# One level of Strassen in the second matrix of layer 0's MLP: seven products of sums of quarters, with the sums on VectorE

## The chip, the cores and the metric

The kernel runs on one core of a Trainium2 chip. The metric is the device time of one execution in microseconds (us), 2352.38 us in the median of two runs before the change (2352.35 and 2352.41). The engines that matter here are TensorE (PE in the profile, with its weight loads as PEld), VectorE (DVE), ScalarE (ACT) and the queue of SyncE (SP), which issues the loads.

## The reference, cut to what matters

The program is a chain of a two-layer block on 256 tokens (a dilated attention mixer, a convolution mixer, each with an MLP) and of a second two-layer block that carries 256 context tokens beside the 256 tokens. Everything is float32. The stage that is changed is the MLP of the second block's layer 0, which runs on both streams, so on 512 tokens:

```
def sq_relu_mlp(h, w1, b1, w2, b2):     # in effect
    return square(relu(h @ w1 + b1)) @ w2 + b2
# h: 512 x 1024, w1: 1024 x 4096, w2: 4096 x 1024
x = layer_norm(alpha * x + g2 * sq_relu_mlp(x * (1 + sc2) + sh2, w1, b1, w2, b2), ln2_g, ln2_b)
```

The gates `g`, scales `sc` and shifts `sh` of a layer come from a modulation product `silu(c) @ w_mod[l] + b_mod[l]`, a vector times a 1024 x 6144 matrix, for two vectors (tokens and context).

## The kernel before, in words

**Products.** Each float32 operand is split in two parts, high and low, of the type that TensorE takes; a product is then three matmuls, high by high, high by low and low by high (`mm3`, L350 to L352). A weight is loaded as a 128x1024 tile (`w`, L337): a DMA on SP, the high part by a cast on ACT (L343), the low part by a subtraction on DVE (L344). There are four buffers each for raw, high and low tiles.

**The MLP** (`mlp`, L727). The 4096 hidden features are cut in eight chunks of 512. `up(hc)` computes a chunk's hidden features: four weight tiles, each 24 matmuls over 512 tokens into its own PSUM bank, then on ACT relu with bias (L751) and square (L752), and the split into `hh` (ACT, L431) and `hl` (DVE, L432). `down(hc)` multiplies the chunk by its 512 rows of the second matrix: four weight tiles, for two halves of the output columns (`nn`) and four groups of 128 tokens (`j`), 96 matmuls of 512 columns. The order on PE is `up(0)`, then `up(hc+1)` and `down(hc)` by turns.

**What comes out.** After each chunk the eight PSUM banks of 128x512 are added on DVE to the sums `facc` in SBUF (L1677); in the first chunk ACT copies them (L1675). At chunk 6 the sum is multiplied by the gate and added to the residual (`tail`, L1707 and L1710, on DVE), and at chunk 7 the banks of the last product go the same way; then the layer norm and the start of layer 1 follow (`ready`).

**Side work.** Each call of `w` in this stage runs one step of a list of side work (`spin`, with `side_n` = 1). First in it is the scaling of the residual by `alpha` and its bias rows (L955, L956), then the gate rows; after it the modulation product of layer 1 (`mod(1)`, L877 on). The matrix of that is not multiplied on TensorE: a 512 KB tile is loaded, and DVE multiplies each half of it by a scalar per partition and adds it to `macd` (L892), the first of eight on ACT (L890); a product with ones on TensorE then sums the partitions (L901). A step of it is one load and four such operations. These steps are `pinned`: traced so that on each engine they stand behind the weight tile that was issued last. Before layer 1 starts, what is left of the list is drained.

**Order.** Each engine works its queue in order. The order of the queues is found while the kernel is built, by a planner that steps through the traced program with its own estimate of each duration, and takes what is ready by priority, which is the place in the program.

Of the kernel before, what the change touches and what calls it, by code (L numbers as in the profile page):

```python
# [10 lines left out]
F32 = mybir.dt.float32  # L11
F32R = mybir.dt.float32r
BF16 = mybir.dt.bfloat16
AF = mybir.ActivationFunctionType
ALU = mybir.AluOpType
# [6 lines left out]
P = 128  # L22
KT = D // P
# [201 lines left out]
MT = ((1, 1), (5, 5), (0, 0))  # L225
# [9 lines left out]
MG = ((),(),(),(0,1,2),())  # L235

NTS = (0, 1, 0)


class WT:  # L240
# [12 lines left out]
class K:  # L253
# [262 lines left out]
    def mixer_a(self, cx):  # L516
# [136 lines left out]
        for i, _ in enumerate(project(0)):  # L653
            if i == 4:
# [3 lines left out]
                nc.vector.tensor_copy(maskb.rearrange("p q k -> p (q k)"), mf.rearrange("p a b -> p (a b)"))  # L658
            self.tick(NTS[0])
        with self.behind(), self.queued():  # L660
            for j in range(2):
                nc.sync.dma_start(self.res[2 + j], A["x_n"][j])
        for wv in range(4):
# [3 lines left out]
            while parts:  # L667
                for g in list(parts):
                    if next(g, 0) == 0:
                        parts.remove(g)  # L670
                self.tick(NTS[1] if wv < 3 else NTS[2])
        self.ahead = self.norm("norm2_0")
# [51 lines left out]
        o, n = self.vat[name]  # L724
        return self.vs[:, o:o + n]

    def mlp(self, uh, ul, c0, c1, w1, w2, bias, evac, first, mt, ready=None):  # L727

        nc, n = self.nc, c1 - c0

        def up(hc):
            hh = self.t(self.xm, [P, 4, n], "hh", F32R, bufs=2)
            hl = self.t(self.xm, [P, 4, n], "hl", F32R, bufs=2)
            pre = self.tiles([w1[f, 0] for f in range(4)], uh, ul, c0, c1, first) if hc == 0 else []
            if hc == 0 and bias is not None:
                self.side_n = 1
            for c in range(2):
                r = self.t(self.xm, [P, 2, n], "r", bufs=2)
                if n == 256 and hc:
                    pt = self.ps()  # L740
                    pv = [pt[:, 0:256], pt[:, 256:512]]
                else:
                    pv = [p_[:, 0:n] for p_ in pre[c * 2:c * 2 + 2] or [self.ps() for _ in range(2)]]
                if hc:
                    for f in range(2):
                        self.lin_f(pv[f], self.w(w1[hc * 4 + c * 2 + f, 0], 8, 128), 0, uh, ul, c0, c1)
                if bias is None and hc:
                    nc.scalar.activation(r.rearrange("p f t -> p (f t)"), pt, AF.Relu)
                else:
                    for f in range(2):  # L750
                        nc.scalar.activation(r[:, f, :], pv[f], AF.Relu, bias=0.0 if bias is None else bias(hc * 4 + c * 2 + f))  # L751
                nc.scalar.activation(r, r, AF.Square)  # L752
                self.split(hh[:, c * 2:c * 2 + 2, :], hl[:, c * 2:c * 2 + 2, :], r)
                self.tick(mt[min(hc, 1)])
            return hh, hl

        def down(hc, hid):
            groups = [([nn], range(n // P)) for nn in range(2)]
            if hc == 7 and bias is not None:
                groups = [([0, 1], [j, j + 1]) for j in (2, 0)] if n == 512 else [([0, 1], [j]) for j in range(2)]  # L760
            Ws = {}
            for nns, js in groups:
                pts = {(nn, j): self.ps() for nn in nns for j in js}
                for nn in nns:
                    for kc in range(2):
                        if (nn, kc) not in Ws:
                            Ws[nn, kc] = self.w(w2[nn, hc * 2 + kc], 2, 512)
                        if hc == 7 and n == 512 and nn == kc == 1 and js[0] == 0:
                            self.turn(ux, 2)
                        for j in js:  # L770
                            with self.after_tp():
                                self.lin_t(pts[nn, j], Ws[nn, kc], 0, 512, hid[0], hid[1], j * P, k0=kc * 2, first=kc == 0, last=kc == 1)
                if hc == 7 and n == 512 and js[0] == 0:
                    self.turn(ux, 2)
                for nn in nns:
                    for j in js:
                        evac(j, nn, hc, pts[nn, j])
                if hc == 7 and n == 512:
                    ux = ready(js)
                if hc == 7 and nns == [0]:  # L780
                    self.halfway()
                self.tick(mt[min(hc, 1)])

        hid = up(0)
        for hc in range(8):
            nxt = up(hc + 1) if hc < 7 else None
            down(hc, hid)
            hid = nxt

    def mlp1(self, l, u2=None):  # L790
        nc = self.nc
        uh, ul, rs = self.take_norm()
        if u2 is not None:
            self.ncol, self.up = 512, u2
        else:
            self.ahead = self.norm("norm1_1")
        r2 = self.t(self.xp, [P, 2], "r2", bufs=2)
        nc.vector.tensor_tensor(r2, rs, rs, ALU.mult)

        def evac(j, nn, hc, pt):  # L800
            r = self.res[2 + j][:, nn * 512:nn * 512 + 512]
            nc.vector.scalar_tensor_tensor(out=r, in0=pt, scalar=r2[:, j:j + 1], in1=r, op0=ALU.mult, op1=ALU.add)

        self.mlp(uh, ul, 0, 256, self.A[f"m1_{l}"], self.A[f"m2_{l}"], None, evac, BY_HALVES, MT[l])
# [153 lines left out]
    def residual(self, l, toks, G):  # L958

        ss = sorted({j // 2 for j in toks})  # L960
        with self.pinned():
            ag = self.row(self.A["rows"][l * 6 + 1:l * 6 + 2])
            gb = {s: self.row(self.gbd[l][1 - s:2 - s, 1, :]) for s in ss}
        yield
        for j in toks:
            with self.pinned():
                self.residual_step(self.res[j], ag, gb[j // 2])
            yield
        with self.pinned():
            G.update({s: self.gate_row(l, 1, s) for s in ss})  # L970
        yield

    def residual_x(self):
# [625 lines left out]
    def layer(self, l):  # L1599
        nc, tc, A = self.nc, self.tc, self.A  # L1600
        q0 = self.q0 = 0 if l == 0 else 256
        self.nq = 512 - q0
        toks = [0, 1, 2, 3] if l == 0 else [2, 3]
        prev = None if l == 0 else (l - 1) * 6 + 4
        spill = l == 0
        uh, ul = self.u
# [4 lines left out]
        if spill:  # L1611
            gb = {s: self.row(self.gbd[0][1 - s:2 - s, 0, :], 2) for s in range(2)}
# [7 lines left out]
        with tc.tile_pool(name=f"mix{l}", bufs=1) as self.xq:  # L1620
            acc = self.mixer2(l, uh, ul, toks)
# [9 lines left out]
            with tc.tile_pool(name=f"tl{l}", bufs=1) as self.lp:  # L1631
# [9 lines left out]
                u = self.uT()  # L1641
                aff = self.affine(l, 1, self.vecl(f"ln1_g_{l}", 0, KT), self.vecl(f"ln1_b_{l}", 0, KT))
                G = {s: self.gate_row(l, 0, s, 2) for s in sorted({j // 2 for j in toks})}
                ux = self.make_u([1], aff, *u)
                for n in range(2):
                    Ws, pts = {}, {}
# [17 lines left out]
        with ExitStack() as cx:  # L1664
            self.xm = cx.enter_context(tc.tile_pool(name=f"ff{l}", bufs=1))
            self.lp = self.xm
            uh, ul = u
            G = {}
            self.side.insert(0, self.residual(l, toks, G))
            accs = [self.t(self.xm, [P, D], f"facc{j}") for j in toks]  # L1670

            def evac(j, nn, hc, pt):
                a = accs[j][:, nn * 512:nn * 512 + 512]
                if hc == 0:
                    nc.scalar.copy(a, pt)  # L1675
                elif hc < 7:
                    nc.vector.tensor_tensor(a, pt, a, ALU.add)  # L1677
                if hc >= 6:
                    self.tail(toks[j], nn, a if hc == 6 else pt, G[toks[j] // 2])

            if l:
                self.last = [self.t(self.xm, [P, D], f"fin{i}") for i in range(2)]
                for i in range(2):
                    nc.sync.dma_start(self.last[i], A["rows"][10 + i:11 + i].broadcast_to([P, D]))
            def ready(js):

                if l == 0:
                    if js[0] == 2:
                        self.drain_side()
                        self.start(1)  # L1690
                    self.ln(js)
                    if js[0] == 0:
                        self.u_ctx = self.make_u([0], self.aff, *self.u)
                    return self.make_u([1], self.aff, *self.u)
            self.mlp(uh, ul, q0, 512, A[f"w1_{l}"], A[f"w2_{l}"], lambda f: self.vecl(f"b1_{l}", f), evac,
                     self.by_quarters(self.make_u([0], aff, *u)) + [(0, KT, 0, 256)] if l == 0 else self.by_quarters(), MT[2], ready)
            self.side_n = 0
            if l:
                self.finish()
# [93 lines left out]
```

## Time and profile before

| | |
|---|---|
| median of two runs | 2352.38 us |
| profiled execution, its own time | 2352.55 us |
| its span, first to last instruction | 2350.8 us |
| mean granted TensorE clock | 0.989 |
| PE busy | 2278.8 us (97%) |
| DVE busy | 1712.0 us (73%) |
| ACT busy | 1117.2 us (48%) |
| POOL busy | 68.9 us (3%) |
| moved by DMA | 364.73 MB, mean 155 GB/s |

Busy time is the time in which an engine had at least one instruction under way; consecutive instructions of one engine overlap by part of their durations, so that the spacing of starts, not the duration of one, is what an instruction costs in a full queue. Matmuls are pipelined in the same way. A clock of 1.00 is 2.4 GHz, and 0.50 is 1.2 GHz.

### The profile page before, as it was taken

The numbers are of one execution on the slowest core, as the hardware profiler recorded it, in microseconds if no ns is written. First come the engines' busy times: TensorE is split into PE (matmuls) and PEld (weight loads), VectorE is DVE, ScalarE is ACT, GpSimd is POOL, SyncE is SP. The second block draws the span as 40 slices with busy tenths as digits, with TensorE's granted clock in tenths as the row PEclk, the third lists the DMA queues.
The fourth block names the chain that finished last, engine by engine and source line by source line (L and its number), as shares of the span: only waits on it lengthen the run. The fifth ranks groups of instructions, "written<-read, shape, count | busy, mean of one in ns | idle before, by whom it ended". The sixth has DMA issues, their size and how long they took to land.

```text
span 2350.8 us, 35308 instructions
## 1 busy us (share of the span) xinstructions
PE 2278.8 (97%) x13784; PEld 1967.8 (84%) x13796; DVE 1712.0 (73%) x2779; ACT 1117.2 (48%) x1702; POOL 68.9 (3%) x72
## 2 busy tenths in 40 slices
PE   8999989999999999999999999999999999998997
PEld 7989868889999888778777778888889898787996
DVE  6788878977766668985755777677568778776667
ACT  5655545554465444433453326434226543544653
POOL 1011100000000000000000000000000000000000
PEclk9999999999999999999999999999999999999999
DMA  5666546765555543223213735556324344345663
GB/s 199 217 188 191 186 138 225 256 217 191 187 179 186 187 154 111 68 72 94 94 47 106 238 95 179 168 174 197 120 90 150 118 136 127 97 138 180 203 190 115
DMA packets 124743, 364.73 MB, mean 155 GB/s; under 512 B 31840, under 2 KB 33632, under 8 KB 124576
## 3 DMA queue, kind: packets, MB, share of 16 engines
q1 hardware_dynamic: 124576, 362.47, 48.4%
q8 instruction: 108, 1.77, 0.3%
q14 instruction: 59, 0.48, 0.1%
HBM read 357.02 MB, written 3.31 MB: 153 GB/s over the span
## 4 chain that ended last, share of the span: by engine, by line
PE 52%; DVE 5%; issue 1%; ACT 1%; POOL 0%; DVEq 0%; POOLq 0%
PE mm L350 16%; PE mm L351 16%; PE mm L352 15%; PE mm L1437 1%; DVE cy L1149 1%; PE mm L1451 1%; DVE wl L344 1%; PE tp L718 1%; PE mm L1328 1%; PE tp L901 0%; PE tp L1015 0%; PE mm L1286 0%; DVE bst L1037 0%; DVE tl L1707 0%; DVE resb L1710 0%
## 5 line engine op out<-in xcount | busy, mean ns | idle before, releaser
L343 ACT CAST wh<-wr 128x1024 fp32r<-128x1024 f32 (+1 forms) x544 | 566.5, 1044 | 889.7 <-PE mm L351 475.5
L344 DVE TENSOR_TENSOR wl<-wr,wh 128x1024 fp32r<-128x1024 f32 (+1 forms) x544 | 659.3, 1214 | 333.6 <-ACT wh L343 324.8
L351 PE MATMUL mm<-ul,wh 128*128 128x256 f32 (+1 forms) x2224 | 704.5, 319 | 2.6 <-DVE ul L432 1.3
L352 PE MATMUL mm<-uh,wl 128*128 128x256 f32 (+1 forms) x2224 | 704.3, 319 | 2.7 <-DVE wl L344 2.7
L350 PE MATMUL mm<-uh,wh 128*128 128x256 f32 (+1 forms) x2224 | 699.9, 321 | 4.7 <-ACT m_q L1253 1.5
L350 PEld LDWEIGHTS mm<-uh,wh 128*128 128x128 f32 x2224 | 417.0, 190 | 43.1 <-ACT wh L343 5.0
L352 PEld LDWEIGHTS mm<-uh,wl 128*128 128x128 f32 x2224 | 422.3, 190 | 34.9 <-DVE wl L344 3.7
L351 PEld LDWEIGHTS mm<-ul,wh 128*128 128x128 f32 x2224 | 422.5, 190 | 33.9 <-issue 1.8
L351 PE MATMUL mm<-wl,hh 128*128 128x512 f32 x640 | 249.6, 391 | 0.0
L352 PE MATMUL mm<-wh,hl 128*128 128x512 f32 x640 | 249.2, 391 | 0.0
L350 PE MATMUL mm<-wh,hh 128*128 128x512 f32 x640 | 247.6, 391 | 0.0
L892 DVE SCALAR_TENSOR_TENSOR macd<-mr,silu_c,macd 128x512 f32<-128x512 f32 x336 | 238.3, 745 | 7.2 <-DMA mr<-in_w_mod 5.2
L350 PE MATMUL mm<-wh,uh 128*128 128x256 f32 x576 | 165.4, 291 | 2.7 <-ACT qk L575 1.5
L351 PE MATMUL mm<-wl,uh 128*128 128x256 f32 x576 | 163.5, 286 | 1.4 <-DVE wl L344 1.4
L352 PE MATMUL mm<-wh,ul 128*128 128x256 f32 x576 | 163.0, 285 | 0.1
L350 PEld LDWEIGHTS mm<-wh,hh 128*128 128x128 f32 x640 | 120.0, 188 | 28.1 <-issue 3.4
L352 PEld LDWEIGHTS mm<-wh,hl 128*128 128x128 f32 x640 | 120.1, 188 | 26.6 <-issue 0.8
L351 PEld LDWEIGHTS mm<-wl,hh 128*128 128x128 f32 x640 | 120.1, 188 | 26.5 <-DVE hl L432 0.8
L1149 DVE SCALAR_TENSOR_TENSOR cy<-hpad,vecl,cy 128x512 f32<-128x512 f32 (+1 forms) x240 | 136.8, 611 | 0.0
L350 PEld LDWEIGHTS mm<-wh,uh 128*128 128x128 f32 x576 | 108.5, 190 | 9.7 <-issue 4.6
L351 PEld LDWEIGHTS mm<-wl,uh 128*128 128x128 f32 x576 | 109.2, 190 | 3.4 <-DVE wl L344 2.1
L352 PEld LDWEIGHTS mm<-wh,ul 128*128 128x128 f32 x576 | 109.1, 190 | 0.7 <-DVE ul L465 0.3
(292 smaller groups left out, 2817.4 us busy)
## 6 DMA issues: line engine op xcount, KB each, us to landing
wr<-in_m SPq DMA_DIRECT2D x128, 512.0 KB
wr<-in_w SPq DMA_DIRECT2D x128, 512.0 KB
wr<-in_w_in SPq DMA_DIRECT2D x116, 512.0 KB
mr<-in_w_mod SPq DMA_DIRECT2D x96, 512.0 KB
wr<-in_a_wqkv SPq DMA_DIRECT2D x72, 512.0 KB
wr<-in_b_win SPq DMA_DIRECT2D x24, 512.0 KB
wr<-in_w_out SPq DMA_DIRECT2D x16, 512.0 KB
wr<-in_w_uq SPq DMA_DIRECT2D x16, 384.0 KB
```

The lines of the kernel that those rows point to most:

```text
L343: self.last_hi = nc.scalar.copy(hi[:, :n], raw[:, :n]).ins
L344: self.last_lo = nc.vector.tensor_tensor(lo[:, :n], raw[:, :n], hi[:, :n].bitcast(F32), ALU.subtract).ins
L350: mm(out, lh, rh, start=first, stop=False)
L351: mm(out, lh, rl, start=False, stop=False)
L352: self.last_mm = mm(out, ll, rh, start=False, stop=last).ins
L718: nc.tensor.transpose(tp[:, b * P:b * P + P], pm[:, b * P:b * P + P], self.ident)
L892: nc.vector.scalar_tensor_tensor(out=a, in0=raw[:, k], scalar=sc, in1=a, op0=ALU.mult, op1=ALU.add)
L1149: nc.vector.scalar_tensor_tensor(out=ys[ft], in0=src, scalar=wk, in1=ys[ft], op0=ALU.mult, op1=ALU.add)
L1328: nc.tensor.matmul(pn[:, d * 130:d * 130 + 129], dts[d][:, s, i * P:i * P + P], v[:, s, 0:129], start=s == ks[0], stop=s == ks[-1])
L1437: nc.tensor.matmul(sc[:, 0:n * P], qs[hp * 2 + i][:, t * P:t * P + P], ks[:, hp * 2 + i, 0:n * P], start=True, stop=True)
L1451: nc.tensor.matmul(pos[hp][i * 64:i * 64 + 64, t * P:t * P + P], v[:, j, h * 64:h * 64 + 64], pt[i][:, j * P:j * P + P], start=j == 0, sto ...
```

## The change

In layer 0 the MLP goes through a new function `mlp_wide`; layer 1 keeps `mlp`. In chunks 0 to 6 the second product is done by one level of Strassen's scheme. The hidden features of the chunk, 512 tokens by 512 features, and the chunk's 512x1024 part of the second matrix are seen as 2 by 2 quarters: tokens in halves of 256 and features in halves (a raw `r` tile each), rows in halves and columns in halves (a raw weight tile of 128x1024 each). Seven products take the place of eight. For each of them the table `PRODUCTS` gives the quarters of the hidden features and their sum or difference, those of the matrix, and the output quarters to which the product is added or from which it is subtracted.

The sums are taken on the raw float32 quarters by VectorE, five of them on the hidden features (128x512) and five on the matrix (128x1024) in a chunk. The split into high and low parts comes after, on every operand of every product: seven times for the hidden features (128x512) and seven for the matrix. A product fills two PSUM banks (`j`), and each bank goes to one or two output quarters: 24 additions or subtractions a chunk, in the first chunk eight of them as copies on ACT. The raw tiles of the second matrix have four buffers of their own (`wq`). The steps of `up(hc+1)` and the products of `down(hc)` are put in turn as the list `TURNS` says. After chunk 6 the eight output tiles go through `tail` in one block, and chunk 7 is done as before (`down_last`), but from `r` tiles that are split by quarters.

The buffers of the rows for the residual and the gates (`row`) go from five to three. `evac` of layer 1 and the order of layer 1's MLP stay.

```
PRODUCTS = (
    (((0, 0),), None, ((0, 1), (1, 1)), ALU.subtract, ((0, 1, ALU.add, True), (1, 1, ALU.add, True))),
    (((1, 0), (0, 0)), ALU.subtract, ((0, 0), (0, 1)), ALU.add, ((1, 1, ALU.add, False),)),
    ...
)
TURNS = (0, 0, 1, 1, 0, 1, 1, 0, 1, 1, 1)
...
            for i, (qa, opa, qb, opb, outs) in enumerate(PRODUCTS):
                y = quarter(rs, qa[0])
                if opa is not None:
                    y_ = self.t(self.xm, [P, 2, half], "as")
                    nc.vector.tensor_tensor(y_, y, quarter(rs, qa[1]), opa)
                    y = y_
                ah, al = split_a(y)
                ws = [raw(*q) for q in qb]
                w = ws[0]
                if opb is not None:
                    w = self.t(self.xm, [P, 1024], "bs")
                    nc.vector.tensor_tensor(w, ws[0], ws[1], opb)
                bh = self.t(self.wp, [P, 1024], "wh", F32R, bufs=self.wbufs[1])
                bl = self.t(self.wp, [P, 1024], "wl", F32R, bufs=self.wbufs[1])
                self.last_hi = nc.scalar.copy(bh, w).ins
                self.last_lo = nc.vector.tensor_tensor(bl, w, bh.bitcast(F32), ALU.subtract).ins
                W = WT(bh, bl, 2, 512)
                pts = [self.ps() for _ in range(nj)]
                for j in range(nj):
                    self.lin_t(pts[j], W, 0, 512, ah, al, j * P)
                for j in range(nj):
                    for T, nn, op, begin in outs:
                        a = acc(T * nj + j, nn)
                        if hc == 0 and begin:
                            nc.scalar.copy(a, pts[j])
                        else:
                            nc.vector.tensor_tensor(a, a, pts[j], op)
...
        for hc in range(7):
            u, d = up(hc + 1), down(hc, rs)
            for step in TURNS:
                if step:
                    next(d)
                else:
                    rs_ = next(u)
...
-            ag = self.row(self.A["rows"][l * 6 + 1:l * 6 + 2])
-            gb = {s: self.row(self.gbd[l][1 - s:2 - s, 1, :]) for s in ss}
+            ag = self.row(self.A["rows"][l * 6 + 1:l * 6 + 2], 3)
+            gb = {s: self.row(self.gbd[l][1 - s:2 - s, 1, :], 3) for s in ss}
```

## Rows read from the trace of the kernel before

**Rows 1.** The page, busy time of each engine over the whole span.
```profile
PE 2278.8 (97%) x13784; PEld 1967.8 (84%) x13796; DVE 1712.0 (73%) x2779; ACT 1117.2 (48%) x1702; POOL 68.9 (3%) x72
```

**Rows 2.** The page, chain that ended last: shares of the span by engine.
```profile
PE 52%; DVE 5%; issue 1%; ACT 1%; POOL 0%; DVEq 0%; POOLq 0%
```

**Rows 3.** Stretches of layer 0's MLP: busy us, instructions, clock, DMA share and GB/s.
```profile
1435.00:1754.00 319.00, 319.00 (x1438) 261.23 (x1437) 217.66 (x286) 128.91 (x148) 0.00 (x0) 1.00 0.51 158
...
1504.00:1548.00 44.00, 44.00 (x198) 35.50 (x198) 30.46 (x43) 17.54 (x20) 0.00 (x0) 1.00 0.56 170
...
1680.00:1724.00 44.00, 44.00 (x196) 36.45 (x195) 17.84 (x22) 15.00 (x16) 0.00 (x0) 1.00 0.31 97
```

**Rows 4.** Timeline of PE in the stage, first and last of 81 matmul spacings.
```profile
1480.24 0.39 PE L350 MATMUL mm<-wh,hh 128*128 128x512 f32 x1
...
1498.60 0.39 PE L350 MATMUL mm<-uh,wh 128*128 128x512 f32 x1
```

**Rows 5.** Groups of DVE by line and shape, 1400 to 1800 us.
```profile
L344 DVE TENSOR_TENSOR wl<-wr,wh 128x1024 fp32r<-128x1024 f32 x72 | 87.9, 1222 | 73.1 <-ACT wh L343 72.8 <-PE mm L351 0.3
L892 DVE SCALAR_TENSOR_TENSOR macd<-mr,silu_c,macd 128x512 f32<-128x512 f32 x112 | 78.0, 746 | 3.8 <-DMA mr<-in_w_mod 3.8
L1677 DVE TENSOR_TENSOR facc<-mm,facc 128x512 f32<-128x512 f32 x48 | 32.2, 685 | 8.8 <-PE mm L352 8.8
L432 DVE TENSOR_TENSOR hl<-r,hh 128x1024 fp32r<-128x1024 f32 x16 | 19.5, 1223 | 9.8 <-ACT hh L431 9.8
L1710 DVE TENSOR_TENSOR resb<-resb,tl 128x512 f32<-128x512 f32 x20 | 13.2, 683 | 0.1
L432 DVE TENSOR_TENSOR ul<-mt,uh 128x512 fp32r<-128x512 f32 x16 | 10.6, 677 | 0.7 <-ACT uh L431 0.7
L956 DVE TENSOR_TENSOR resb<-resb,row 128x1024 f32<-128x1024 f32 x4 | 4.9, 1221 | 0.0
```

**Rows 6.** Timeline of DVE where its queue was full: start, us, operation, count.
```profile
1439.10 1.22 DVE L344 TENSOR_TENSOR wl<-wr,wh 128x1024 fp32r<-128x1024 f32 x1
1440.24 1.22 DVE L955 SCALAR_TENSOR_TENSOR resb<-resb,row 128x1024 f32<-128x1024 f32 x1
...
1579.46 4.05 DVE L892 SCALAR_TENSOR_TENSOR macd<-mr,silu_c,macd 128x512 f32<-128x512 f32 x6
...
1736.87 1.28 DVE L1707 TENSOR_TENSOR tl<-facc,row 128x512 f32<-128x512 f32 x2
1738.07 0.69 DVE L1677 TENSOR_TENSOR facc<-mm,facc 128x512 f32<-128x512 f32 x1
...
1754.32 1.28 DVE L1707 TENSOR_TENSOR tl<-mm,row 128x512 f32<-128x512 f32 x2
```

**Rows 7.** Who waited for whom on DVE, 1435 to 1760: total, times, longest.
```profile
DVE wl L344 <- ACT wh L343: 72.2, 37, 4.5
...
DVE macd L892 <- DMA mr<-in_w_mod: 3.8, 3, 2.7
```

**Rows 8.** Groups of ACT by line and shape, 1400 to 1800 us.
```profile
L343 ACT CAST wh<-wr 128x1024 fp32r<-128x1024 f32 x72 | 75.7, 1054 | 197.9 <-PE mm L352 99.4 <-PE mm L351 88.7 <-DMA wr<-in_w 6.2
L751 ACT ACTIVATE r<-mm,vecl 128x512 f32<-128x512 f32 x32 | 21.9, 683 | 1.3 <-DVE hl L432 1.3
...
L431 ACT CAST uh<-mt 128x512 fp32r<-128x512 f32 x16 | 9.5, 619 | 7.8 <-DVE mt L1022 7.6
```

**Rows 9.** The stretch of layer 0's mixer in which DVE is fullest, by 50 us.
```profile
950.00:1000.00 50.00, 46.38 (x229) 37.13 (x229) 47.99 (x109) 20.03 (x41) 1.54 (x1) 1.00 0.18 59
1000.00:1050.00 50.00, 47.02 (x229) 37.86 (x228) 46.07 (x117) 20.03 (x41) 3.36 (x2) 0.97 0.24 74
```

**Rows 10.** A stretch of layer 1 in which PE stops and goes, by 5 us.
```profile
2065.00:2070.00 5.00, 2.67 (x20) 2.15 (x17) 3.41 (x7) 0.79 (x3) 0.00 (x0) 1.00 0.50 161
2070.00:2075.00 5.00, 4.40 (x25) 4.19 (x23) 4.00 (x8) 1.67 (x3) 0.00 (x0) 0.66 0.01 3
...
2085.00:2090.00 5.00, 5.00 (x45) 5.00 (x44) 4.78 (x11) 2.87 (x5) 0.00 (x0) 1.00 0.30 98
```

More of the change, by code (lines that the diff above doesn't have):

```diff
@@ L237 @@
 NTS = (0, 1, 0)
+PRODUCTS = (
+    (((0, 0),), None, ((0, 1), (1, 1)), ALU.subtract, ((0, 1, ALU.add, True), (1, 1, ALU.add, True))),
+    (((1, 0), (0, 0)), ALU.subtract, ((0, 0), (0, 1)), ALU.add, ((1, 1, ALU.add, False),)),
+    (((1, 0), (1, 1)), ALU.add, ((0, 0),), None, ((1, 0, ALU.add, True), (1, 1, ALU.subtract, False))),
+    (((0, 0), (1, 1)), ALU.add, ((0, 0), (1, 1)), ALU.add, ((0, 0, ALU.add, True), (1, 1, ALU.add, False))),
+    (((0, 0), (0, 1)), ALU.add, ((1, 1),), None, ((0, 0, ALU.subtract, False), (0, 1, ALU.add, False))),
+    (((1, 1),), None, ((1, 0), (0, 0)), ALU.subtract, ((0, 0, ALU.add, False), (1, 0, ALU.add, False))),
+    (((0, 1), (1, 1)), ALU.subtract, ((1, 0), (1, 1)), ALU.add, ((0, 0, ALU.add, False),)),
+)
+TURNS = (0, 0, 1, 1, 0, 1, 1, 0, 1, 1, 1)
 class WT:
@@ L725, in cst_vec, with mlp @@
         return self.vs[:, o:o + n]
-    def mlp(self, uh, ul, c0, c1, w1, w2, bias, evac, first, mt, ready=None):
+    def mlp(self, uh, ul, c0, c1, w1, w2, bias, evac, first, mt):
         nc, n = self.nc, c1 - c0
@@ L759, in down @@
             if hc == 7 and bias is not None:
-                groups = [([0, 1], [j, j + 1]) for j in (2, 0)] if n == 512 else [([0, 1], [j]) for j in range(2)]
+                groups = [([0, 1], [j]) for j in range(2)]
             Ws = {}
@@ L767, in down @@
                             Ws[nn, kc] = self.w(w2[nn, hc * 2 + kc], 2, 512)
-                        if hc == 7 and n == 512 and nn == kc == 1 and js[0] == 0:
-                            self.turn(ux, 2)
                         for j in js:
@@ L772, in down @@
                                 self.lin_t(pts[nn, j], Ws[nn, kc], 0, 512, hid[0], hid[1], j * P, k0=kc * 2, first=kc == 0, last=kc == 1)
-                if hc == 7 and n == 512 and js[0] == 0:
-                    self.turn(ux, 2)
                 for nn in nns:
@@ L777, in down @@
                         evac(j, nn, hc, pts[nn, j])
-                if hc == 7 and n == 512:
-                    ux = ready(js)
                 if hc == 7 and nns == [0]:
@@ L788, in mlp, with mlp_wide, up, quarter @@
             hid = nxt
+    def mlp_wide(self, uh, ul, w1, w2, bias, accs, result, parts, mt, ready):
+        nc = self.nc
+        half, nj = 256, 2
+        first, n, c0, c1 = parts, 512, 0, 512
+        acc = lambda j, nn: accs[j][:, nn * 512:nn * 512 + 512]
+        def up(hc):
+            rs = []
+            pre = self.tiles([w1[f, 0] for f in range(4)], uh, ul, c0, c1, first) if hc == 0 else []
+            if hc == 0:
+                self.side_n = 1
+            for c in range(2):
+                r = self.t(self.xm, [P, 2, n], "r", bufs=4)
+                pv = pre[c * 2:c * 2 + 2] or [self.ps() for _ in range(2)]
+                for f in range(2):
+                    if hc:
+                        self.lin_f(pv[f], self.w(w1[hc * 4 + c * 2 + f, 0], 8, 128), 0, uh, ul, c0, c1)
+                    if f == 0:
+                        yield
+                for f in range(2):
+                    nc.scalar.activation(r[:, f, :], pv[f], AF.Relu, bias=bias(hc * 4 + c * 2 + f))
+                nc.scalar.activation(r, r, AF.Square)
+                rs.append(r)
+                self.tick(mt[min(hc, 1)])
+                yield rs
+        def quarter(rs, q):
+            return rs[q[1]][:, :, q[0] * half:q[0] * half + half]
+        def split_a(src):
+            ah = self.t(self.xm, [P, 2, half], "ah", F32R, bufs=3)
+            al = self.t(self.xm, [P, 2, half], "al", F32R, bufs=3)
+            self.split(ah, al, src)
+            return ah, al
+        def down(hc, rs):
+            Bs = {}
+            def raw(kc, nn):
+                if (kc, nn) not in Bs:
+                    Bs[kc, nn] = t = self.t(self.xm, [P, 1024], "wq", bufs=4)
+                    self.last_w = nc.sync.dma_start(t, w2[nn, hc * 2 + kc].rearrange("p k f -> p (k f)")).ins
+                    self.spin(self.side_n)
+                return Bs[kc, nn]
+            for i, (qa, opa, qb, opb, outs) in enumerate(PRODUCTS):
[23 more added lines that the diff above has]
+                            nc.scalar.copy(a, pts[j])
+                        else:
+                            nc.vector.tensor_tensor(a, a, pts[j], op)
+                if i in (2, 6):
+                    self.tick(mt[min(hc, 1)])
+                yield
+        def down_last(rs):
+            Ws, nns = {}, [0, 1]
+            for js in ([2, 3], [0, 1]):
+                hid = [split_a(quarter(rs, (js[0] // 2, kc))) for kc in range(2)]
+                pts = {(nn, j): self.ps() for nn in nns for j in js}
+                for nn in nns:
+                    for kc in range(2):
+                        if (nn, kc) not in Ws:
+                            Ws[nn, kc] = self.w(w2[nn, 14 + kc], 2, 512)
+                        if nn == kc == 1 and js[0] == 0:
+                            self.turn(ux, 2)
+                        for j in js:
+                            with self.after_tp():
+                                self.lin_t(pts[nn, j], Ws[nn, kc], 0, 512, *hid[kc], j % 2 * P, first=kc == 0, last=kc == 1)
+                if js[0] == 0:
+                    self.turn(ux, 2)
+                for nn in nns:
+                    for j in js:
+                        result(j, nn, pts[nn, j])
+                ux = ready(js)
+                self.tick(mt[1])
+        for rs in up(0):
+            pass
+        for hc in range(7):
[3 more added lines that the diff above has]
+                    next(d)
+                else:
+                    rs_ = next(u)
+            for _ in d:
+                pass
+            rs = rs_
+        for j in range(4):
+            for nn in range(2):
+                result(j, nn, acc(j, nn))
+        down_last(rs)
@@ L961, in residual @@
         with self.pinned():
-            ag = self.row(self.A["rows"][l * 6 + 1:l * 6 + 2])
-            gb = {s: self.row(self.gbd[l][1 - s:2 - s, 1, :]) for s in ss}
+            ag = self.row(self.A["rows"][l * 6 + 1:l * 6 + 2], 3)
+            gb = {s: self.row(self.gbd[l][1 - s:2 - s, 1, :], 3) for s in ss}
         yield
@@ L969, in residual @@
         with self.pinned():
-            G.update({s: self.gate_row(l, 1, s) for s in ss})
+            G.update({s: self.gate_row(l, 1, s, 3) for s in ss})
         yield
@@ L1670, in layer, with result @@
             accs = [self.t(self.xm, [P, D], f"facc{j}") for j in toks]
+            def result(j, nn, src):
+                self.tail(toks[j], nn, src, G[toks[j] // 2])
             def evac(j, nn, hc, pt):
@@ L1678, in evac @@
                 if hc >= 6:
-                    self.tail(toks[j], nn, a if hc == 6 else pt, G[toks[j] // 2])
+                    result(j, nn, a if hc == 6 else pt)
             if l:
@@ L1685, in ready @@
             def ready(js):
[L1687 to L1696, printed above, removed]
+                if js[0] == 2:
+                    self.drain_side()
+                    self.start(1)
+                self.ln(js)
+                if js[0] == 0:
+                    self.u_ctx = self.make_u([0], self.aff, *self.u)
+                return self.make_u([1], self.aff, *self.u)
+            bias = lambda f: self.vecl(f"b1_{l}", f)
+            if l == 0:
+                self.mlp_wide(uh, ul, A["w1_0"], A["w2_0"], bias, accs, result,
+                              self.by_quarters(self.make_u([0], aff, *u)) + [(0, KT, 0, 256)], MT[2], ready)
+            else:
+                self.mlp(uh, ul, q0, 512, A["w1_1"], A["w2_1"], bias, evac, self.by_quarters(), MT[2])
             self.side_n = 0
```

## The prediction, on record before the changed kernel ran

> **What bounds the kernel now.** The busy times of the whole span come first [rows 1]: PE 97%, DVE 73%, ACT 48%. The chain that ended last agrees [rows 2]: most of it is PE, DVE has 5%. Averages don't decide a change in one stage, so the next view is that stage alone, 1435 to 1754 us, from the first weight tile of layer 0's MLP to the last sums of chunk 6 [rows 3]. There PE is busy for all 319.0 us at the full clock (1.00, so 2.4 GHz), while DVE is busy 217.7 us and idle 101.3, and ACT is busy 128.9. So PE sets the time, and a matmul saved here is time saved, as long as DVE stays under PE. How much DVE has left is the question. The chunk rows show that it isn't spread evenly: 30.5 of 44 us while the modulation product of layer 1 runs beside the MLP, 17.8 after it has ended [rows 3]. Most of DVE's idle time is the wait for ACT's cast before the low part is subtracted, 72.2 us in 37 waits [rows 7]: it was early and waited for the pace that PE sets. That is spare time, but no more than 101 us of it.
>
> **What PE saves.** 81 matmuls of 512 columns take 1498.60 - 1480.24 = 18.36 us, 0.2267 us each [rows 4]. Seven products of 12 matmuls stand for eight of 12 (two token groups, two parts of 128 rows, three matmuls), so a chunk falls from 192 to 180 matmuls, 43.5 to 40.8 us. Seven chunks save 84 x 0.2267 = 19.0 us. That is the most that the change can give, 0.8% of the kernel.
>
> **What DVE gets.** I price an instruction by the spacing of starts in a full queue. A two-tensor operation of 128x1024 costs 1440.24 - 1439.10 = 1.14 us; six multiply-adds of 128x512 take 4.05 us with the last at its full 0.75, so 0.66 each; two of 128x512 start 1.20 us apart from their successor, so 0.60 each [rows 6]. The operations that the change adds are all of these two shapes: low parts, PSUM sums, and sums of two SBUF tiles, whose single durations are alike (1222 and 1221 ns, 677 to 685 ns) whether the source is PSUM or SBUF and the target fp32r or float32 [rows 5]. So no term needs a guess at an operation that the trace lacks.
>
> A chunk before: 8 low parts of weights (9.1), 2 of hidden features (2.3), 8 adds (4.8): 16.2 us. A chunk after: 4 + 7 low parts of weights (12.5), 5 sums of weight quarters (5.7), 5 sums of hidden quarters (3.0), 7 low parts of these (4.2), 24 adds (14.4): 39.8 us. The first chunk has 8 copies on ACT both times. So each of seven chunks asks 23.6 us more of DVE, 165 us in all, where 101 were idle.
>
> Beside this stands work that the change leaves: 112 multiply-adds of the modulation [rows 5] (73.9 us), eight passes over the residual (9.1), the eight outputs of chunk 6, two operations each (9.6), some 4 us of small ones. With 60 low parts of weights (68.2), 16 of hidden features (18.2) and 48 adds (28.8), the stage before comes to 212 us, near the 218 that the profile has as busy. After: 212 + 165 = 377 us of DVE. PE would need 300. **DVE becomes the bound of the stage**: a chunk with the modulation beside it asks about 58 us of DVE against 40.8 of PE, and one without it 39.8.
>
> **How tightly DVE packs.** At no idle time the end of chunk 6 is 377 us after 1435, at 1812 instead of 1754: +58 us. The trace has no full stretch of this kind. From below: in the stretch where DVE is fullest, among dependent small operations, it is busy 94.1 of 100 us [rows 9]. Nine tenths is my estimate for worse packing, since the chain of a product goes DVE, ACT, DVE, PE, DVE. I take 0.94, the nearest row: 377 / 0.94 = 401 us, +82. At 0.90 it is 419, +100.
>
> **Other edits.** *ACT*: a chunk has 11 casts of 1.05, 4 relus of 0.68, 2 squares at the cast's 1.05 and 7 casts of 0.62 [rows 8], 20.7 us, hidden under DVE. *Loads*: still eight weight tiles a chunk, and the DMA share is 0.51 [rows 3]. The new raw tiles stay until the fourth quarter is used, so the second raw tile of the next chunk is loaded late; the two weight tiles of `up` at the head of the order (10.9 us of PE) cover it. Without the cover each chunk would wait about as long as the longest wait on a load, 2.7 us [rows 7], so 0 to 19 us; I take 0. *Three row buffers instead of five*: the gate rows' loads on SP wait until the residual is scaled, and the weight loads stand behind them; 0, or at most those eight passes, 9 us. It is once per layer, and layer 1 uses only three rows; I take 0. *The block of outputs after chunk 6*: PE's last chunk needs low parts that in program order stand behind these 9.6 us and the last sums of 2.4. Before, they were spread. Between -9.6 (all beside chunk 7's matmuls) and +13; I take 0, as the outputs of quarters that are done early can go ahead.
>
> **The clock.** In a stretch of layer 1 where PE has work for only 2.67 of 5 us, the granted clock of the next 5 us is 0.66 and it is back at 1.00 when PE is full again [rows 10], that is, part of the time at 1.2 GHz. In the fullest DVE stretch 3 to 4 us of idle PE in 50 left it at 1.00 and 0.97 [rows 9]. Here PE would idle about a quarter of the stage. I price this at 0, since PE at 40.8 us a chunk has 17 to spare under DVE's 58; only a fall in the last two chunks would show.
> The Trainium skill, "TensorE: Matmul & The Clock Gate", section "Why this matters for your kernels", speaks against such a change: it advises against idle gaps between bursts of matmuls, because the clock then goes back to its low level. The trace agrees in its small stop-and-go stretch. By that rule alone every product could run at the low clock, which is the second rival below.
>
> **The sum.** The profiled execution took 2352.55 us (span 2350.8 and 1.7 around it), within 0.2 of the median. 2352.5 + 82 = **2435 us**, 3.5% slower; the 19 us of PE are inside the 82, since the new end is counted from DVE.
>
> **Rivals.**
> *It comes out not slower.* The place is the modulation's 74 us on DVE. If the planner lets them slip behind the products, they would have to run after chunk 6; layer 1 needs only a part of them at once. Then DVE has 377 - 74 = 303 us for PE's 300, and the time is about 2352.5 - 19 + 3, some 2337 us, up to 2355 with stalls. It decides as soon as over 58 us of DVE's work can leave the stage. Against it: each step is pinned behind a weight tile, DVE works in order, and the list is drained before layer 1. For it: only that DVE's queue was seen to give adds and multiply-adds turns. 6%.
> *DVE binds, and the chain of a product shows, with the low clock on top.* A product without overlap costs a sum of 1.22, a cast of 1.05, a low part of 1.22, 12 matmuls of 0.2267 (2.7, or 5.4 at 1.2 GHz) and about 3.4 adds (2.1): 8.3 or 11.0 us, against 5.0 of DVE's own (35.2 in 7). If half of the 49 products stall DVE for that difference, 24 x 3.3 = 79 us or 24 x 6.0 = 144 come to the +58: 2490 to 2555. For it: one buffer each for the two kinds of sums, and rows 10. Against it: the work of `up` and the modulation lies between, low parts have four buffers and a product two banks of six. 16%.
> *DVE binds less than I count*: close packing, outputs hidden behind chunk 7. +58 - 9.6 = +48: 2400. Below 2400 I see 6% more, beside the first rival.
>
> **How the numbers follow.** The forecast has 72%: DVE binds and packs at 0.90 to 1.00. Its range is 2400 to 2352.5 + 100 + 13 + 19 = 2485. The range to give is this one, 2400 to 2485: below it lie the first rival and the last (12%), above it most of the second, so that some 2 in 10 are outside, counting that part of the second falls within. 2%, 47 us, is about what a measurement of this kernel can tell from no change. Faster by over 2% can't come from 19 us: 1%. Within 2%, up to 2399: 12%. Slower: 87%.
>
> **What would show it.** In the stage, DVE above 90% busy and PE near 300 us of 390 to 410, with PE's waits on the low parts (`wl`) and the split halves (`al`), or for banks that DVE has not emptied; 84 matmuls fewer in all. DVE's total goes up by some 165 us. After the modulation ends, a chunk should take about 41 to 44 us instead of 58. The clock should be under 1.00 in some stretches of the first five chunks. I am wrong if multiply-adds of the modulation are found after chunk 6, if sums of SBUF tiles start clearly less than 0.6 us apart, or if DVE idles over 10% of the stage while PE waits.

## The result, and the profile after

The changed kernel takes 2415.6 us in the median (2414.0 to 2417.2), the kernel before 2352.4: a ratio of 1.0268, 95% interval [1.0251, 1.0285], so 63 us more. Forecast were 2435 us, in 2400 to 2485. The profiled execution has a span of 2415.1 us.

First the page of the changed kernel: busy times, and the chain that ended last by engine.

```profile
PE 2293.7 (95%) x13712; PEld 1952.6 (81%) x13712; DVE 1872.1 (78%) x3019; ACT 1148.0 (48%) x1760; POOL 67.9 (3%) x72
...
PE 42%; DVE 15%; issue 2%; ACT 1%; DMA 0%; DVEq 0%; POOL 0%; SPq 0%
```

Against [rows 1, 2], DVE is busy for 160 us more, where 165 were counted by spacing, and its share of the chain goes from 5% to 15%. The stage is the next view; stretches of it as in [rows 3]: PE, PEld, DVE, ACT and POOL busy, then the clock.

```profile
1435.00:1817.00 382.00, 344.09 (x1390) 254.71 (x1390) 377.06 (x525) 159.85 (x207) 0.00 (x0) 0.97 0.39 126
1504.00:1562.00 58.00, 50.72 (x195) 35.27 (x194) 56.39 (x79) 22.29 (x28) 0.00 (x0) 0.97 0.41 132
1765.00:1804.00 39.00, 35.81 (x154) 28.11 (x153) 39.00 (x69) 19.23 (x24) 0.00 (x0) 1.00 0.18 57
```

The roles are exchanged. Before, PE was busy for all of the stage and DVE for 218 of 319 us [rows 3]; now DVE is busy for 377.1 of 382 us, and PE has gaps. The third row is a stretch of chunk 6, with no modulation beside it: DVE is full there too, while PE is busy for 35.8 of 39 us. The first tail operation on a bank of chunk 7, from DVE's timeline:

```profile
1817.27 1.28 DVE L1842 TENSOR_TENSOR tl<-mm,row 128x512 f32<-128x512 f32 x2
```

Before it started at 1754.32 us [rows 6], 63 us earlier: the whole difference arises before this point.

The groups of DVE, 1400 to 1870 us: count, busy us and mean ns.

```profile
L874 DVE TENSOR_TENSOR facc<-facc,mm 128x512 f32<-128x512 f32 x160 | 102.9, 682 | 1.0 <-ACT facc L872 0.7
L1020 DVE SCALAR_TENSOR_TENSOR macd<-mr,silu_c,macd 128x512 f32<-128x512 f32 x112 | 81.3, 747 | 0.1
...
L859 DVE TENSOR_TENSOR bs<-wq,wq 128x1024 f32<-128x1024 f32 x35 | 42.7, 1220 | 1.4 <-DMA wq<-in_w 1.4
L863 DVE TENSOR_TENSOR wl<-bs,wh 128x1024 fp32r<-128x1024 f32 x35 | 42.7, 1220 | 0.5 <-ACT wh L862 0.5
...
L852 DVE TENSOR_TENSOR as<-r,r 128x512 f32<-128x512 f32 x21 | 14.4, 687 | 0.0
```

160 adds, 35 sums of 128x1024, and the durations of [rows 5]: no operation costs more than its neighbour of before. And the waits are gone. DVE idled 72 us for ACT's casts of weights [rows 7]; now it is 3.4, from 1435 to 1850 us (total, times, longest):

```profile
DVE wl L359 <- ACT wh L358: 2.9, 1, 2.9
...
DVE wl L863 <- ACT wh L862: 0.5, 2, 0.3
```

It is PE that waits, in the same stretch:

```profile
PE mm L365 <- ACT ah L446: 17.2, 13, 2.3
PE tp L1143 <- ACT resb L1180: 11.3, 1, 11.3
PE mm L367 <- DVE al L447: 6.7, 6, 3.3
PE mm L366 <- DVE wl L863: 5.5, 4, 2.5
```

The first is a wait for the high part of hidden features or of their sum, which ACT casts behind DVE's sum. The second is one wait at the end, for the layer norm behind the last outputs. The pace of the chunks is read on ACT, from the square of the first half of each next chunk; first the kernel before, then the changed one, from the start of chunk 2's products to the start of chunk 6's (starts in us):

```profile
1541.45 1.06 ACT L752 ACTIVATE r<-r 128x1024 f32<-128x1024 f32 x1
...
1717.99 1.06 ACT L752 ACTIVATE r<-r 128x1024 f32<-128x1024 f32 x1
```

```profile
1553.36 1.06 ACT L822 ACTIVATE r<-r 128x1024 f32<-128x1024 f32 x1
...
1608.04 1.07 ACT L822 ACTIVATE r<-r 128x1024 f32<-128x1024 f32 x1
...
1658.03 1.06 ACT L822 ACTIVATE r<-r 128x1024 f32<-128x1024 f32 x1
...
1712.15 1.06 ACT L822 ACTIVATE r<-r 128x1024 f32<-128x1024 f32 x1
...
1770.60 1.06 ACT L822 ACTIVATE r<-r 128x1024 f32<-128x1024 f32 x1
```

50 to 58 us a chunk, 54 in the mean, against 44.1 before. At the last of these squares the changed kernel is 52.6 us behind (1770.60 against 1717.99), at the first tail operation on chunk 7 63: some 10 us arise in chunk 6 and its outputs.

### The profile page after: what moved, and what is told of

Read it like the earlier page. It is cut to its first block, busy times and chain, and to the rows that moved or that the text cites. A ratio compares the mean times of both kernels' runs of the same rounds, so it can differ in the third digit from the quotient of the medians.

```text
span 2415.1 us, 35470 instructions
## 1 busy us (share of the span) xinstructions
PE 2293.7 (95%) x13712; PEld 1952.6 (81%) x13712; DVE 1872.1 (78%) x3019; ACT 1148.0 (48%) x1760; POOL 67.9 (3%) x72
## 4 chain that ended last, share of the span: by engine, by line
PE 42%; DVE 15%; issue 2%; ACT 1%; DMA 0%; DVEq 0%; POOL 0%; SPq 0%
PE mm L365 12%; PE mm L367 12%; PE mm L366 12%; DVE facc L874 3%; DVE macd L1020 2%; DVE wl L359 2%; DVE wl L863 1%; PE mm L1565 1%; DVE cy L1277 1%; PE mm L1579 1%; DVE bs L859 1%; DVE al L447 1%; PE tp L733 1%; PE mm L1456 1%; DVE as L852 1%
## 5 line engine op out<-in xcount | busy, mean ns | idle before, releaser
L358 ACT CAST wh<-wr 128x1024 fp32r<-128x1024 f32 (+1 forms) x516 | 536.8, 1044 | 709.5 <-PE mm L366 384.9
L359 DVE TENSOR_TENSOR wl<-wr,wh 128x1024 fp32r<-128x1024 f32 (+1 forms) x516 | 625.2, 1214 | 265.3 <-ACT wh L358 255.2
L365 PEld LDWEIGHTS mm<-uh,wh 128*128 128x128 f32 x2224 | 416.6, 190 | 44.8 <-issue 4.7
L366 PE MATMUL mm<-wl,hh 128*128 128x512 f32 x384 | 150.1, 392 | 0.0
L367 PE MATMUL mm<-wh,hl 128*128 128x512 f32 x384 | 149.8, 392 | 0.0
L365 PE MATMUL mm<-wh,hh 128*128 128x512 f32 x384 | 148.0, 393 | 0.0
L365 PE MATMUL mm<-wh,ah 128*128 128x512 f32 x228 | 88.1, 411 | 18.4 <-ACT ah L446 17.2
L874 DVE TENSOR_TENSOR facc<-facc,mm 128x512 f32<-128x512 f32 x160 | 102.9, 682 | 1.0 <-ACT facc L872 0.7
L366 PE MATMUL mm<-wl,ah 128*128 128x512 f32 x228 | 89.8, 407 | 6.1 <-DVE wl L863 5.5
```

The lines of the kernel that those rows point to most:

```text
L358: self.last_hi = nc.scalar.copy(hi[:, :n], raw[:, :n]).ins
L359: self.last_lo = nc.vector.tensor_tensor(lo[:, :n], raw[:, :n], hi[:, :n].bitcast(F32), ALU.subtract).ins
L365: mm(out, lh, rh, start=first, stop=False)
L366: mm(out, lh, rl, start=False, stop=False)
L367: self.last_mm = mm(out, ll, rh, start=False, stop=last).ins
L874: nc.vector.tensor_tensor(a, a, pts[j], op)
```

## The experiments

Theory A: VectorE's work sets the stage. Rival B: the chain of a product (DVE, ACT, DVE, PE, DVE), or TensorE's low clock between its bursts, sets it. All differences below are ratios to the kernel before, less one, times 2352.4 us; the changed kernel is at +63.0.

| run | ratio, 95% interval | us against before |
|---|---|---|
| changed, modulation left out | 1.0020 [1.0011, 1.0030] | +4.7 |
| before, modulation left out | 1.0002 [0.9992, 1.0011] | +0.5 |
| changed, an eighth product | 1.0290 [1.0274, 1.0306] | +68.2 |
| changed, sums on GpSimd | 1.0340 [1.0321, 1.0359] | +80.0 |
| modulation left out, six chunks | 0.9999 [0.9990, 1.0008] | -0.2 |
| chunks 0, 2, 4 | 1.0103 [1.0087, 1.0118] | +24.2 |
| six chunks, 0 to 5 | 1.0266 [1.0248, 1.0283] | +62.6 |
| chunk 5 only | 1.0026 [1.0016, 1.0037] | +6.1 |
| no chunk | 1.0037 [1.0024, 1.0051] | +8.7 |
| no chunk, outputs spread | 0.9994 [0.9985, 1.0004] | -1.4 |
| chunk 5 only, outputs spread | 1.0003 [0.9995, 1.0012] | +0.7 |
| changed, outputs spread | 1.0273 [1.0258, 1.0287] | +64.2 |

**Work of DVE that no product waits for.** In both kernels:

```
-                                else:
+                                elif l == 0 or sec < 2:
                                     nc.vector.scalar_tensor_tensor(out=a, in0=raw[:, k], scalar=sc, ...)
```

> The changed kernel without the 112 multiply-adds of layer 1's modulation that fall in the stage (the last four of its six sections keep only the part that ScalarE computes, so these gates and shifts are wrong; its loads stay). If VectorE's sum of work sets the stage, 74 to 78 us of it go: VectorE needs some 303 us where TensorE needs 300, and the time falls from 2415 to 2335 to 2350 us, below the kernel before. If the chain of a product (sum, cast, low part, matmuls, adds) or the low clock sets it, this work, which is in no chain of a product, is worth little: 2395 to 2415 us.

> The kernel before with the same 112 multiply-adds left out. TensorE sets its stage, so both theories say no change: 2345 to 2353 us. If this falls as much as the changed kernel does, the multiply-adds cost time by themselves and tell nothing of VectorE as the bound.

The kernel before doesn't move; the changed one falls by 58 us. That is what theory A says: these 112 operations lie in no product's chain and cost nothing while PE is the bound. But A's number was missed: 2357 us, not 2335 to 2350, and not below the kernel before. Two stretches of that run:

```profile
1435.00:1719.00 284.00, 284.00 (x1233) 223.68 (x1233) 265.84 (x346) 144.14 (x187) 0.00 (x0) 1.00 0.50 160
...
1759.00:1769.00 10.00, 4.61 (x12) 3.20 (x12) 10.00 (x18) 1.04 (x1) 0.00 (x0) 0.77 0.19 58
```

PE is booked as busy throughout, yet starts 1233 matmuls in 284 us, 0.230 us each, where 1438 in 319 us were 0.222 [rows 3]. A matmul is booked for 0.39 us and the next can start after 0.227, so gaps under 0.16 us don't show. By this count some 10 us go in small gaps (an estimate, as some records can be missing), and more at the end of the stage, while DVE is full. The squares on ACT agree: from the first in the stage to that of the first half of chunk 7's features this run takes 273.5 us and the kernel before 279.2, where six chunks should save 16; from there to the first tail operation on chunk 7 it takes 48.0 against 36.3.

**More work for PE.**

```
                 for j in range(nj):
-                    self.lin_t(pts[j], W, 0, 512, ah, al, j * P)
+                    for _ in range(2 if i == 3 else 1):
+                        self.lin_t(pts[j], W, 0, 512, ah, al, j * P)
```

> The changed kernel with the fourth product's twelve matmuls computed twice in each of seven chunks, so TensorE has as much to do as before the change (84 matmuls, 19.0 us more), VectorE nothing more. If VectorE sets the stage: 2415 us, at most 4 us more. If TensorE's work or its clock still sets it: 2434 us, or less than 2415 us if the fuller TensorE keeps a higher clock and the clock was what cost time.

The 84 matmuls that the change saves come back at 5 us instead of 19 (the two intervals overlap, so 5 is uncertain too). In that run's stage PE is 12 us busier and DVE as full as before:

```profile
1435.00:1820.00 385.00, 356.47 (x1470) 274.20 (x1469) 375.88 (x523) 161.65 (x206) 0.00 (x0) 0.96 0.40 125
```

The saving of the seven products is worth almost nothing while DVE is the bound.

**The sums off DVE.** Both `nc.vector.tensor_tensor` of the sums become `nc.gpsimd.tensor_tensor`.

> The changed kernel with the ten sums of quarters of each chunk, 35 of 128x1024 and 35 of 128x512, on GpSimd in place of VectorE. By VectorE's sum of work 61 us go from it: 316 us against TensorE's 300, so 2350 to 2362 us, if GpSimd is fast enough and doesn't disturb VectorE. Price of GpSimd unknown: at over 5 us for a 128x1024 sum it would become the bound of the chunk (five of them and five halves against 41 us). If the chain of a product sets the time, slower sums make it longer: over 2415 us.

17 us slower than the changed kernel, with 61 us of work taken from DVE. The groups of DVE and of POOL in this run, 1400 to 1850 us:

```profile
L1020 DVE SCALAR_TENSOR_TENSOR macd<-mr,silu_c,macd 128x512 f32<-128x512 f32 x112 | 115.9, 1061 | 0.0
L874 DVE TENSOR_TENSOR facc<-facc,mm 128x512 f32<-128x512 f32 x160 | 102.8, 674 | 0.0
L359 DVE TENSOR_TENSOR wl<-wr,wh 128x1024 fp32r<-128x1024 f32 x39 | 65.8, 1691 | 5.0 <-ACT wh L358 4.7 <-PE mm L366 0.3
```

```profile
L859 POOL TENSOR_TENSOR bs<-wq,wq 128x1024 f32<-128x1024 f32 x35 | 97.2, 2778 | 105.1 <-DVE wl L863 96.1 <-DMA wq<-in_w 9.0
L852 POOL TENSOR_TENSOR as<-r,r 128x512 f32<-128x512 f32 x21 | 34.4, 1636 | 80.8 <-DVE al L447 80.8
```

GpSimd isn't the bound (it idles on DVE), and B's longer sum, 2.8 us for 1.2, isn't the price either, for DVE has no idle time. DVE's own operations grew: the multiply-adds from 747 to 1061 ns and these low parts from 1220 to 1691, 35 and 18 us for these two groups alone (difference of the means by count), some 70 with the others. The adds that read PSUM stayed at 674. Single operations show why; DVE's timeline, then GpSimd's:

```profile
1499.98 3.38 DVE L359 TENSOR_TENSOR wl<-wr,wh 128x1024 fp32r<-128x1024 f32 x1
...
1513.50 3.04 DVE L359 TENSOR_TENSOR wl<-wr,wh 128x1024 fp32r<-128x1024 f32 x1
...
1524.70 1.27 DVE L874 TENSOR_TENSOR facc<-facc,mm 128x512 f32<-128x512 f32 x2
```

```profile
1499.48 2.81 POOL L859 TENSOR_TENSOR bs<-wq,wq 128x1024 f32<-128x1024 f32 x1 [1.76 <-DVE wl L863]
...
1513.06 2.40 POOL L859 TENSOR_TENSOR bs<-wq,wq 128x1024 f32<-128x1024 f32 x1 [2.43 <-DVE wl L863]
...
1524.85 2.41 POOL L859 TENSOR_TENSOR bs<-wq,wq 128x1024 f32<-128x1024 f32 x1 [4.82 <-DVE wl L863]
```

Each of the two low parts starts while a sum runs on GpSimd and ends 1.1 us after it (1503.36 against 1502.29 us, 1516.54 against 1515.46), which is nearly its whole duration of 1.22. The two adds with an input in PSUM take their usual 1.27 us beside the third sum. So operations with two SBUF inputs take turns with GpSimd's, and the work moved came back on DVE. Up to chunk 6 the run keeps level with the changed kernel (its last such square starts at 1767.39 us), but 15 multiply-adds of the modulation are left over, 16.3 us, that the changed kernel has behind it by then. From that square to the first tail operation on chunk 7 it takes 64.2 us against 46.7, and that is the 17.
The Trainium skill, "GPSIMD Engine Reference", section "Specifications", says that GpSimd shares its SBUF interfaces with VectorE, with contention where a VectorE instruction has two SBUF inputs; this run agrees and gives the size.

**Which chunks pay, and the frame.** A function for a chunk of eight products, `down_plain`, made like `down_last`, lets a set of chunks (`CHUNKS`) take seven; in further runs the outputs of chunk 6 are written as they come:

```
+            if hc not in CHUNKS:
+                for rs_ in up(hc + 1):
+                    pass
+                down_plain(hc, rs)
+                rs = rs_
+                continue
...
+                        if hc == 6:                       # spread
+                            result(j, nn, acc(j, nn))
...
-        for j in range(4):
-            for nn in range(2):
-                result(j, nn, acc(j, nn))
```

> The changed kernel's frame without any chunk in seven products: hidden features split by quarters, the outputs of chunk 6 in one block, three row buffers, raw tiles kept longer, but eight products in each chunk. Both theories put this at the kernel before, 2350 to 2356 us. More than that is the price of the frame, which would then be a part of the 63 us that the sums don't explain.

> The frame without any chunk in seven products, with the outputs of chunk 6 written as soon as each of its banks is added, not in one block after the chunk. The frame cost 8.9 us, and TensorE was idle for some 7 us at its end, behind the layer norm that waits for VectorE's outputs. If that block is the whole price of the frame, this is the kernel before again: 2350 to 2354 us. If split quarters, buffers or order cost it, 2357 to 2361 us as without the spreading.

The frame alone costs 8.7 us, which neither theory had; with the outputs spread it costs nothing. PE's stretch and its longest wait with the outputs in one block, then the same stretch and PE's only wait from 1700 us with them spread:

```profile
1763.00:1773.00 10.00, 2.55 (x12) 1.78 (x10) 10.00 (x21) 2.66 (x3) 0.60 (x2) 0.88 0.50 158
```

```profile
PE tp L1168 <- ACT resb L1205: 8.4, 2, 7.6
```

```profile
1763.00:1773.00 10.00, 8.32 (x53) 7.06 (x52) 10.00 (x16) 5.85 (x9) 0.00 (x0) 1.00 0.40 130
```

```profile
PE tp L1172 <- ACT resb L1209: 2.0, 2, 1.7
```

DVE is full in both; the block puts eight tiles of chunk 6 ahead of what the layer norm waits for.

> The changed kernel, seven chunks in seven products, with each output of chunk 6 written right after the last product that touches it. VectorE's sum stays, so the sum alone says 2412 to 2416 us; if the price of the frame (8.9 us) is an addition of its own to VectorE's excess, 2406 to 2409 us.

In the changed kernel the spreading brings nothing. The price of the block isn't an addition to DVE's excess: where DVE is full for the whole stage, the order of its work is no longer what costs.

> Seven products in chunks 0 to 5, eight in chunk 6, outputs in one block. VectorE has 23.6 us less to do than in the changed kernel. If its sum of work sets the end: 2391 to 2395 us. If chunk 6, which has no modulation beside it, was near TensorE's own 40.8 us already, only the backlog at its end goes: 2403 to 2412 us.

No difference that can be measured, though DVE has 23.6 us less to do: the 2391 to 2395 us of the sum over the stage, as A used it, are missed. Its chunks keep the changed kernel's pace up to the end of the modulation:

```profile
1551.94 1.06 ACT L822 ACTIVATE r<-r 128x1024 f32<-128x1024 f32 x1
...
1768.46 1.06 ACT L822 ACTIVATE r<-r 128x1024 f32<-128x1024 f32 x1
```

216.5 us for four chunks, 217.2 in the changed kernel. Then DVE has time to spare and can make up nothing, as PE is the bound of chunk 6:

```profile
1769.00:1799.00 30.00, 30.00 (x134) 24.82 (x133) 14.43 (x32) 9.82 (x13) 0.00 (x0) 1.00 0.31 94
```

So most of the loss, the 52.6 us, is in chunks 0 to 5, with the modulation beside them. What seven products in chunk 6 cost by themselves is less sure. With PE as the bound the block of outputs has its price again (PE waits 8.4 us for the layer norm, as in the frame, and 11.3 in the changed kernel), so it may hide a part of what chunk 6 gained; six chunks with the outputs spread were not run.

> Seven products in chunks 0, 2 and 4 only, with the modulation beside them; the others take eight products. Over the stage VectorE's work is 212 + 71 = 283 us, less than TensorE's 311. If only the sum over the stage counts, as the prediction had it, VectorE can catch up in the chunks between: 2344 to 2352 us. If VectorE binds chunk by chunk (few buffers, so a late VectorE stops TensorE at once and lost time is not made up), each of the three costs 58 - 43.5 = 14.5 us: 2385 to 2400 us.

Between the two: +15.5 us over the frame, 5 a chunk, not 0 and not 14.5. Stretches of it:

```profile
1479.00:1523.00 44.00, 44.00 (x188) 33.65 (x187) 38.77 (x55) 16.10 (x20) 0.00 (x0) 1.00 0.61 197
...
1567.00:1611.00 44.00, 39.42 (x151) 29.10 (x152) 37.27 (x49) 17.21 (x21) 0.00 (x0) 0.92 0.61 193
```

In the second stretch DVE isn't full, and PE has gaps all the same. By the squares the three chunks aren't alike: chunk 0 takes 42.2 us, chunk 2 55.2 and chunk 4 48.2, where the frame takes 43.5, 44.8 and 43.7. So DVE can make up a part in a chunk of eight products that follows; why these chunks differ so much stays open.

> The first experiment (112 multiply-adds of layer 1's modulation left out, gates and shifts wrong) with seven products in chunks 0 to 5 only; chunk 6 takes the old eight, with 8 adds. The first experiment kept TensorE at work until 1720 us and lost some 11 us after it, while VectorE was full. If that was VectorE's backlog at the end (three products in a row, 24 adds, 16 output operations), the backlog is gone here: 2.7 us more of TensorE, 11 or more less of waiting, so about 2345 us. If the loss of that experiment is spread over all chunks in small gaps of TensorE, it shrinks by a seventh only: 2354 to 2358 us.

2352 us is 5 below the seven chunks, so the end of chunk 6 was a part of that loss, and between the two expectations. Against the frame it is 9 us less, of which chunks 0 to 5 give 6 by the squares (272.8 us against 279.2): freed of the modulation, six chunks of seven products bring a part of their 16 us, at most about half. The frame without the modulation was not run.

> Seven products in chunk 5 only, the one that in the kernel before has no multiply-adds of the modulation beside it and isn't the last before the outputs. VectorE needs 39.8 us there against 40.8 of TensorE. If VectorE's work in that chunk decides: 2.7 us less than the kernel before, 2348 to 2351 us, the only version here that could beat it. If the chain of a product costs by itself, 2355 us or more.

> Seven products in chunk 5 only, with chunk 6's outputs spread. Without the spreading it took 2.7 us off TensorE and 4 us off the frame, but the frame cost 9. If the frame's price goes with the block: 2347 to 2350 us, some 2.7 us under the kernel before, the first version that beats both. If not: 2353 to 2357 us.

In one block the time is 2.6 us under the frame, but the two intervals overlap; the 2355 us or more of the chain of a product are reached by the frame's price alone. With the outputs spread, 2351 us lie between the two expectations, no different from the kernel before nor clearly from the spread frame. A saving of 2.7 us is not seen; where it goes stays open. No version tried beats the kernel before beyond its interval.

## Why the prediction was right, and where its size was off

**The bound.** Right: DVE from 218 of 319 us to 377 of 382, PE with gaps, and the leave-out pair shows cause and not only coincidence, -58 us in one kernel and 0 in the other. The page has 84 weight loads fewer than [rows 1] (and 72 matmuls, as some of their records can be missing).

**DVE's sum.** Right: 377 counted, 377.06 busy. Every term went by spacing in a full queue [rows 6], not by single durations [rows 5], and no operation came out dearer. (The busy time of the stage rose by 159 and not by 165, since the queue before had gaps and booked more operations at their full duration: 217.66 us, 212 by spacing.)

**Packing.** This step was mis-sized. I took 0.94 from a stretch of many small operations [rows 9]; it was 377.06 / 382 = 0.987. With that the working gives +63 instead of +82. DVE hardly waits for its own chain (3.4 us on casts of weights): there was another product, weight tile or multiply-add to take. PE was booked for 344 us, not near 300; 1390 matmuls of 0.2267 are 315 (an estimate), and the booking hides small gaps. Its longest sum of waits was for the high parts (`ah`, 17.2 us), which the prediction's list lacks, ahead of `al` and `wl`.

**Sum over the stage.** Right in total, wrong as a rule. Most of the loss, 52.6 us, is in the chunks with the modulation. Of these 58 us were counted against 40.8 of PE; chunks 2 to 5 took 54, as the multiply-adds spread over 290 us (starts from 1463.6 to 1753.9) where they took 198 before (1463.4 to 1661.8). Chunk 6, put at 39.8 us of DVE, comes to 46.7 from its square to the first tail operation on chunk 7, with the outputs of 9.6. The sum fits because DVE is full in both parts; in the run with six chunks, where DVE has time to spare in chunk 6, it is 17 us or more too low.

**The block of outputs.** Put at 0 within -9.6 to +13: 8.7 us where PE is the bound; in the changed kernel, spreading it brings nothing.

**Loads, row buffers.** 0 was right: DVE waits for a raw tile once, 1.4 us, before its first sum at 1430 us, and not in the stage; and the frame with its outputs spread, which has the three row buffers, is level with the kernel before.

**The clock.** It fell as expected in part of the stage, here by 20 us:

```profile
1560.00:1580.00 20.00, 16.42 (x66) 11.37 (x65) 20.00 (x33) 9.11 (x12) 0.00 (x0) 1.00 0.32 105
1580.00:1600.00 20.00, 16.57 (x57) 11.54 (x58) 20.00 (x28) 6.14 (x8) 0.00 (x0) 0.83 0.55 184
```

DVE is full in both, PE's idle time comes first, and 84 matmuls more, at a mean clock of 0.96, cost 5 us: the low clock is not what sets the time.

**The rivals.** The multiply-adds of the modulation did slip, by 92 us, but no further than 1753.9 us, before chunk 6, so the change could not come out level. Without them the time is 2357 us, just above the 2337 to 2355 of the rival: its price was nearly right for work that leaves the stage. That they could run after it at no cost was not tested. The chain with the low clock, 2490 us or more, is refuted by DVE's 98.7%.

## What to carry to other kernels

An algorithm that saves matmuls pays in element operations: weigh it by the engine that gets them, in the stretch where it gets them, with the other work of that stretch. Here 2.7 us of TensorE a chunk cost 23.6 us of VectorE. Look for the side work that was free as long as VectorE had time, and check a change that only rearranges the frame by itself, since it can cost or save as much as the idea.

## What the runs showed of the hardware that was not expected

VectorE operations with two SBUF inputs stretch while GpSimd works on SBUF: the low parts of 128x1024 weight tiles that are split as loaded (L359) from 1220 to 1691 ns and a 128x512 multiply-add from 747 to 1061 in the mean, an add with a PSUM input not at all (682 and 674 ns). In the rows shown a low part that meets a GpSimd sum ends 1.1 us after the sum does, so the two take turns. Other groups, which meet fewer of them, grew less (low parts of sums of weights from 1220 to 1345 ns). GpSimd itself took 2.8 us for a 128x1024 sum and 1.6 for a 128x512 one in the mean, its own waits for a turn included, against 1.22 and 0.69 on VectorE.
